# Weight tiles that move on by 16 bytes in SBUF, and up projection tiles streamed backwards

## The chip, the core and the metric

The kernel runs on one core of one Trainium2 chip. The metric is device time in microseconds (us). Three runs of the kernel before gave 872.74, 875.40 and 876.86 us; the median, 875.4 us, is what the prediction is held against. One more execution was profiled.

## The reference

One layer of a diffusion backbone on 512 latent tokens of 1024 channels, with 256 context tokens that only feed the start states of the retention branch. Cut to what matters here:

```python
u = modulate(x, sh1, sc1)                       # layer norm, then adaLN shift and scale
mix = token_mixer(u @ w_in, ...)                # retention and pooling branches, gates, @ w_out
x = post_norm(ALPHA * x + g1 * mix, ln1_g, ln1_b)
u2 = modulate(x, sh2, sc2)
h = (u2 @ w_up).reshape(B, 8, 64, 2 * 2816)     # up projection: 44 feature tiles of 128
h = conv3x3_depthwise(h) + conv_b               # nine taps for every channel
a, b = split(h)
x = post_norm(ALPHA * x + g2 * ((gelu(a) * b) @ w_down), ln2_g, ln2_b)
```

All arithmetic is float32.

## The kernel before, in words

**Split products.** A float32 product is made of three matmuls in the type float32r. A weight tile of 128 rows and 1024 columns is loaded into a buffer `raw`; `split` (L86 to L91) makes two tiles of it: ScalarE (ACT) casts `raw` to `hi` (L89), and VectorE (DVE) or GpSimd (POOL) writes the rest, `lo = raw - hi` (the subtraction stands in a helper, L84). The activations are split in the same way beforehand. `mm3` (L93 to L96) then issues hi by hi (L94), hi by lo (L95) and lo by hi (L96), all summed in one PSUM bank. The tags `hi` and `lo` have two buffers each, which take turns, so every tile of such a tag starts at one of two addresses.

**What uses them.** `feature_mm` (L383) makes one output tile of 128 features by 512 tokens: eight steps over the contraction, 24 matmuls of 512 columns, the weights stationary and the activations streamed. The tiles of the projections for gates and pooling, of the branch projections and most of the up projection are stationary in that way. In the value projection and in most of the down projection the `hi` and `lo` tiles are the streamed side instead. The first stage (`g0_mm`, L339) takes its weights from the same two tags, through a line of its own (L323).

**The order of the work.** Most of the program stands in an order written by hand. In the up projection, the loop near L1001 goes over 44 tiles `i`: it prepares the weights of tile `i + 2` (`up_prep`; each third tile is split into spare room, not into `hi` and `lo`), runs the matmuls of tile `i` (`up_mm`, which calls `feature_mm` for tiles 6 to 43; the first six tiles were prepared earlier and are made in halves of 256 columns), and then starts the 3x3 convolution on the PSUM bank: the centre tap on ACT (L1010), two taps by ACT and POOL (L1013, L936), six by DVE (`tap`, L938). After each second tile there is gelu on ACT, the product of the pair on DVE (`gated`, L987), and the split of the product for the down projection (`act_out`, L991 and L84). There are eight PSUM banks; a bank is free again when the last tap has read it. The down projection follows; its first two weight tiles already need all eight banks.

**Names and lines that matter.** `split` L86, `mm3` L93, `feature_mm` L383, `out_x` L802 (which borrows buffers of the tags `hi` and `lo` for rows of x), `up_mm` L962, `kernel` L1188.

Of the kernel before, what the change touches and what calls it, by code (L numbers as in the profile page):

```python
# [9 lines left out]
F32 = mybir.dt.float32  # L10
F32R = mybir.dt.float32r
# [3 lines left out]
P = 128  # L15
D = 1024
# [4 lines left out]
NKT = D // P  # L21
# [25 lines left out]
def layer_kernel(ctx: ExitStack, tc: tile.TileContext, a: dict):  # L47
    nc = tc.nc
    act, dve, pool, pe, dma = nc.scalar, nc.vector, nc.gpsimd, nc.tensor, nc.sync

    sb = ctx.enter_context(tc.tile_pool(name="sb", bufs=1))
# [5 lines left out]
    def nm(s):  # L57
        count[0] += 1
        return f"{s}_{count[0]}"

    def slot(i, shape, dt=F32):
        return sb.tile(shape, dt, tag=f"S{i}", name=nm(f"S{i}"))
# [7 lines left out]
    def t2(shape=(P, SEQ), dt=F32):  # L70
        return sb.tile(list(shape), dt, tag="t2", bufs=8, name=nm("t2"))
# [8 lines left out]
    def bank():  # L80
        return ps_pool.tile([P, SEQ], F32, tag="ps", name=nm("ps"))

    def sub(eng, out, x, y):
        eng.tensor_tensor(out, x, y, ALU.subtract)  # L84

    def split(raw, shape, eng):  # L86
        hi = sb.tile(list(shape), F32R, tag="hi", bufs=2, name=nm("hi"))
        lo = sb.tile(list(shape), F32R, tag="lo", bufs=2, name=nm("lo"))
        act.copy(hi, raw)  # L89
        sub(eng, lo, raw, hi.bitcast(F32))  # L90
        return hi, lo  # L91

    def mm3(out, sh, sl, mh, ml, first, last):  # L93
        pe.matmul(out, lhsT=sh, rhs=mh, start=first, stop=False)  # L94
        pe.matmul(out, lhsT=sh, rhs=ml, start=False, stop=False)  # L95
        pe.matmul(out, lhsT=sl, rhs=mh, start=False, stop=last)  # L96

    def load(t, src):
        dma.dma_start(t, src)
        return t  # L100
# [63 lines left out]
    def prep(i):  # L164
        _, src, shape, eng = steps[i]
        if src is None:
            return ()
        raw = raw4(shape)
        if isinstance(src, list):
            for k, one in enumerate(src):  # L170
                load(raw[:, k, :], one)
        else:
            load(raw, src)
        return split(raw, shape, eng)
# [30 lines left out]
    def finish_mod(m, j, scale):  # L205
        dve.tensor_scalar(m[:, j:j + 1], m[:, j:j + 1], bada[:, j:j + 1], 1.0 if scale else 0.0, ALU.add, ALU.add)
# [5 lines left out]
    NF0 = (4 + N_G0) * P  # L212
# [39 lines left out]
    def first_prep(kt, raw):  # L252
        w = split(raw, (P, NF0), pool)
        first_mod(kt)
        modulate(mod, kt, 8 + kt, xnT[:, kt, :], uh[:, kt, :], ul[:, kt, :], pool)
        return w
# [63 lines left out]
    finish_mod(mod, 0, False)  # L320
    matvec(8, ada_slot(8), junk)
    finish_mod(mod, 8, True)
    wh, wl = (sb.tile([P, NF0], F32R, tag=t, bufs=2, name=nm(t)) for t in ("hi", "lo"))  # L323
    act.activation(uh[:, 0, :], xnT[:, 0, :], AF.Identity, bias=mod[:, 0:1], scale=mod[:, 8:9])
    for cs, cp in ((lo_half, dve.tensor_copy), (hi_half, act.copy)):
        cp(wh[:, cs], raw0[:, cs])
# [15 lines left out]
    for kt in range(NKT):  # L342
        wh, wl = ready
        if kt == 0:
            g0 = [bank() for _ in range(4)]
            g0_mm(kt, range(0, 4), range(2))
            held += [x_trans(2, 1), x_trans(3, 1)]
            g0_mm(kt, range(0, 4), range(2, 3))
            for h in held:
                act.copy(*h)  # L350
            g0 += [bank() for _ in range(N_G0)]
            ready = split(first_load(1), (P, NF0), pool)
            first_mod(1)
            modulate(mod, 1, 9, xnT[:, 1, :], uh[:, 1, :], ul[:, 1, :], pool)
        elif kt + 1 < NKT:
            ready = first_prep(kt + 1, first_load(kt + 1))
        if kt:
            g0_mm(kt, range(0, 4))
        g0_mm(kt, range(4, 4 + N_G0))
        if kt == 1:  # L360
            silu_cc = load(row(), a["c_ctx"].broadcast_to([P, D]))
        elif kt == 2:
            for hf in range(2):
                cs = slice(hf * SEQ, (hf + 1) * SEQ)
                t = t2()
                act.activation(t, silu_cc[:, cs], AF.Sigmoid)
                dve.tensor_tensor(silu_cc[:, cs], silu_cc[:, cs], t, ALU.mult)
        if kt >= 6:
            load(ctx_raw[:, kt - 6, :], a["ctx"][(kt - 6) * P:(kt - 5) * P, :])
        if kt >= 4:  # L370
            ctx_mod(kt - 4)
# [8 lines left out]
        act.activation(s, ps, AF.Sigmoid)  # L380
        dve.tensor_tensor(gs[:, f, :], ps, s, ALU.mult)

    def feature_mm(wh, wl, nkt, mh, ml):  # L383
        ps = bank()
        for kt in range(nkt):
            mm3(ps, wh[:, kt, :], wl[:, kt, :], mh[:, kt, :], ml[:, kt, :], kt == 0, kt == nkt - 1)
        return ps

    def feature_step(src, nkt, mh, ml, post, eng):
        step(lambda wh, wl: post(feature_mm(wh, wl, nkt, mh, ml)), src, (P, nkt, P), eng)  # L390
# [347 lines left out]
    def br_step(t):  # L738
        def body(wh, wl):
            if t == 0:  # L740
                m1[0] = slot(1, [P, NKT, SEQ])
            ps = feature_mm(wh, wl, NKT, zs[0], zs[1])
            dve.tensor_tensor(m1[0][:, t, :], ps, sg[0][:, t, :], ALU.mult)
            for n in [n for n in range(4) if BR_W[n] == t]:
                prep_out(*divmod(n, 2))

        step(body, a["w_br"][t], (P, NKT, P), dve)

    def bp_step(t):
        def body(wh, wl):  # L750
            if t == 0:
                mm_[0] = slot(2, [P, NKT, SEQ], F32R)
                mm_[1] = slot(5, [P, NKT, SEQ], F32R)
            ps = feature_mm(wh, wl, 4, poolT[:, 0], poolT[:, 1])
            m = t2()
            dve.tensor_tensor(m, ps, sg[1][:, t, :], ALU.mult)
            dve.tensor_tensor(m, m, m1[0][:, t, :], ALU.add)
            act.copy(mm_[0][:, t, :], m)
            sub(pool, mm_[1][:, t, :], m, mm_[0][:, t, :].bitcast(F32))
            for n in [n for n in range(4) if BP_W[n] == t]:  # L760
                prep_out(*divmod(4 + n, 2))

        step(body, a["w_bp"][t], (P, 4, P), dve)
# [25 lines left out]
    mh, ml = mm_  # L789
# [7 lines left out]
    u2h = slot(1, [P, NKT, SEQ], F32R)  # L797
    u2l = slot(8, [P, NKT, SEQ], F32R)

    xr, stats, early = {}, {}, []  # L800

    def out_x(tb):  # L802
        t = xr[tb] = sb.tile([P, D], F32, tag="lo" if tb % 2 else "hi", bufs=2, name=nm("xr"))
        load(t, a["x"][tb * P:(tb + 1) * P, :])
        return act.activation(t, t, AF.Copy, scale=ALPHA)

# [52 lines left out]
    def half(i, hf):  # L859
        ps, wh, wl = early[i]  # L860
        hs = slice(hf * CTX, (hf + 1) * CTX)
        for kt in range(NKT):
            mm3(ps[:, hs], wh(kt), wl(kt), u2h[:, kt, hs], u2l[:, kt, hs], kt == 0, kt == NKT - 1)
# [28 lines left out]
    for tb in range(2):  # L892
        tc.keep_in_program_order(out_x(tb))
# [4 lines left out]
    out_mm(1)  # L898
    out_tr(0)
    out_x(2)  # L900
    early_prep(0, dve)
    out_norm(1)
    out_mm(2)
    out_tr(1)
    out_x(3)
    early_prep(1, dve)
    out_norm(2, lambda: early_prep(2, pool))
# [54 lines left out]
    def up_mm(i):  # L962
        if i < n_early:
            half(i, 1)
            return early[i][0]
        wh, wl = prepped.pop(i)
        return feature_mm(wh, wl, NKT, u2h, u2l)

    srcs, accs = {}, {}

# [29 lines left out]
    for i in range(2 * NFF):  # L1000
        up_prep(i + 2)  # L1001
        ps = up_mm(i)
        if i >= 2 * NFF - 2:
            src = t2()
            act.copy(src, ps)
        else:
            src = ps
        srcs[i] = src
        acc = accs[i] = t2()
        act.activation(acc, src, AF.Identity, bias=convb[:, i:i + 1], scale=convw[:, i, 4:5])  # L1010
        for n in POOL_TAPS:
            hs = t2()
            act.activation(hs, src, AF.Copy, scale=convw[:, i, n:n + 1])  # L1013
            tap(acc, hs, None, *TAPS[n])
        gens = [conv_taps(i, DVE_TAPS[:3])]
        if i:
            gens.insert(0, conv_taps(i - 1, DVE_TAPS[3:]))
        weave(*gens)
        settle(i - 1)
        if i >= 3 and i % 2 == 1:  # L1020
            act_out((i - 3) // 2)
    down0 = down_prep(0, pool)
    i = 2 * NFF - 1
# [29 lines left out]
    for f in range(2, N_FRONT):  # L1053
# [5 lines left out]
        if f >= N_FRONT - 8 and f % 2 == 0:  # L1059
            i = (f - N_FRONT + 8) // 2  # L1060
# [144 lines left out]
```

## Time and profile before

| what | value |
|---|---|
| median of three runs | 875.4 us (872.74 to 876.86) |
| the profiled execution's own time | 874.79 us |
| its span, first to last instruction | 873.0 us |
| TensorE (PE) busy | 821.6 us, 94% |
| VectorE (DVE) busy | 624.4 us, 72% |
| GpSimd (POOL) busy | 444.2 us, 51% |
| ScalarE (ACT) busy | 366.2 us, 42% |
| granted TensorE clock, mean | 0.981 of full |

The profile is of one execution. Busy shares are averages over stages with different limits, so each stage is read by itself. A matmul's own duration overlaps its neighbours' (the array is a pipeline), so its pace is read from the distance of starts. A profile line carries the engine, the line of the program, the operation, the tiles it writes and reads, and shapes; "idle before" names what ended the engine's wait.

### The profile page before, as it was taken

How to read it: one execution, taken by the hardware profiler on the slowest of the kernel's cores; microseconds unless marked ns; L12 is line 12 of the kernel's file. 1: busy time of each engine (PE TensorE's matmuls, PEld its weight loads, DVE VectorE, ACT ScalarE, POOL GpSimd, SP SyncE). 2: the span in 40 equal slices, each digit the busy share in tenths (PEclk: the TensorE clock that was granted, in tenths of full speed). 3: DMA queues.
4: the chain of work that ended last, by engine and by line, in shares of the span. 5: the costliest groups of instructions: out<-in, count | busy, mean ns of one | idle time of the engine just before them, and what ended most of it. 6: DMA issues, size and time to landing. Idle time of an engine off the chain costs nothing.

```text
span 873.0 us, 10556 instructions
## 1 busy us (share of the span) xinstructions
PE 821.6 (94%) x3865; PEld 678.5 (78%) x3865; DVE 624.4 (72%) x959; ACT 366.2 (42%) x575; POOL 444.2 (51%) x304
## 2 busy tenths in 40 slices
PE   6889989999999999998998899999999998799993
PEld 4667878778888888887787898888888776688883
DVE  7899996676267773346757769999999999612138
ACT  4434544121444343233335476666655565223200
POOL 4877411121543230113456878899888886212245
PEclk9999999999999999999999999999999999999997
DMA  9932466767221104344503312222222252224202
GB/s 352 345 105 94 127 207 218 236 226 216 72 73 49 50 1 145 100 154 163 196 1 121 121 50 84 86 96 99 96 97 95 75 169 83 87 97 144 73 1 96
DMA packets 33780, 106.94 MB, mean 122 GB/s; under 512 B 4528, under 2 KB 5312, under 8 KB 33728
## 3 DMA queue, kind: packets, MB, share of 16 engines
q1 hardware_dynamic: 33728, 106.27, 35.6%
q8 instruction: 30, 0.49, 0.2%
q14 instruction: 22, 0.18, 0.1%
HBM read 104.14 MB, written 2.11 MB: 122 GB/s over the span
## 4 chain that ended last, share of the span: by engine, by line
PE 40%; DVE 39%; POOL 8%; DMA 6%; issue 5%; ACT 2%; SPq 0%; DVEq 0%; POOLq 0%; ACTq 0%
DVE t L938 19%; PE ps L96 11%; PE ps L95 11%; PE ps L94 11%; DVE S L84 4%; DMA raw<-in_wada 4%; DVE t L987 3%; POOL lo L84 3%; DVE raw L203 2%; DVE lo L84 2%; PE ps L339 1%; POOL S L84 1%; POOL sm L123 1%; PE ps L608 1%; DVE sm L130 1%
## 5 line engine op out<-in xcount | busy, mean ns | idle before, releaser
L96 PE MATMUL ps<-S,lo 128*128 128x512 f32 (+1 forms) x544 | 212.2, 392 | 5.1 <-DVE lo L84 4.7
L94 PE MATMUL ps<-S,hi 128*128 128x512 f32 (+1 forms) x544 | 213.6, 393 | 2.7 <-ACT hi L89 2.7
L95 PE MATMUL ps<-S,hi 128*128 128x512 f32 (+1 forms) x544 | 212.5, 391 | 0.2 <-POOL S L84 0.2
L84 POOL TENSOR_TENSOR lo<-raw,hi 128x1024 fp32r<-128x1024 f32 (+1 forms) x53 | 134.0, 2530 | 107.2 <-ACT hi L89 105.3
L938 DVE SCALAR_TENSOR_TENSOR t<-ps,convw,t 128x441 f32<-128x441 f32 (+1 forms) x252 | 167.6, 693 | 15.8 <-POOL t L936 11.5
L89 ACT CAST hi<-raw 128x1024 fp32r<-128x1024 f32 (+1 forms) x98 | 98.9, 1009 | 168.2 <-PE ps L95 61.7
L96 PEld LDWEIGHTS ps<-S,lo 128*128 128x128 f32 x544 | 102.8, 189 | 29.8 <-DVE lo L84 6.8
L94 PEld LDWEIGHTS ps<-S,hi 128*128 128x128 f32 x544 | 103.6, 190 | 23.7 <-ACT hi L89 3.1
L936 POOL TENSOR_TENSOR t<-t,t 128x448 f32<-128x448 f32 x88 | 116.7, 1329 | 10.0 <-ACT t L1013 6.2
L95 PEld LDWEIGHTS ps<-S,hi 128*128 128x128 f32 x544 | 103.7, 191 | 21.3 <-POOL S L84 0.6
L95 PE MATMUL ps<-S,S 128*128 128x512 f32 (+1 forms) x308 | 113.8, 370 | 5.4 <-DVE S L84 5.0
L94 PE MATMUL ps<-S,S 128*128 128x512 f32 (+1 forms) x308 | 113.1, 369 | 3.6 <-DVE t L938 3.6
L96 PE MATMUL ps<-S,S 128*128 128x512 f32 (+1 forms) x308 | 113.8, 370 | 0.2 <-POOL S L84 0.2
L84 DVE TENSOR_TENSOR lo<-raw,hi 128x1024 fp32r<-128x1024 f32 (+1 forms) x47 | 61.4, 1307 | 53.0 <-ACT hi L89 53.0
L84 POOL TENSOR_TENSOR S<-raw,S 128x1024 fp32r<-128x1024 f32 x21 | 50.8, 2423 | 68.7 <-ACT S L735 44.5
L95 PE MATMUL ps<-lo,S 128*128 128x512 f32 x208 | 81.6, 392 | 0.7 <-DVE lo L84 0.6
L96 PE MATMUL ps<-hi,S 128*128 128x512 f32 x208 | 81.3, 391 | 0.0
L94 PE MATMUL ps<-hi,S 128*128 128x512 f32 x208 | 79.2, 392 | 0.0
L95 PEld LDWEIGHTS ps<-S,S 128*128 128x128 f32 x308 | 58.9, 191 | 15.6 <-DVE S L84 5.5
L94 PEld LDWEIGHTS ps<-S,S 128*128 128x128 f32 x308 | 58.6, 191 | 13.6 <-DVE t L938 4.0
L96 PEld LDWEIGHTS ps<-S,S 128*128 128x128 f32 x308 | 58.9, 191 | 10.4 <-POOL S L84 1.1
L84 POOL TENSOR_TENSOR S<-t,S 128x512 fp32r<-128x512 f32 (+1 forms) x29 | 44.8, 1557 | 31.2 <-DVE t L220 11.1
(205 smaller groups left out, 1187.3 us busy)
## 6 DMA issues: line engine op xcount, KB each, us to landing
raw<-in_w_up SPq DMA_DIRECT2D x44, 512.0 KB, 3.3
raw<-in_wada SPq DMA_DIRECT2D x32, 512.0 KB, 4.2
raw<-in_w_down SPq DMA_DIRECT2D x22, 512.0 KB, 3.3
S<-in_wada SPq DMA_DIRECT2D x16, 512.0 KB, 6.8
raw<-in_w_first SPq DMA_DIRECT2D x8, 512.0 KB, 7.4
raw<-in_w_v SPq DMA_DIRECT2D x16, 256.0 KB, 3.3
raw<-in_w_ga SPq DMA_DIRECT2D x8, 512.0 KB, 3.4
raw<-in_w_gb SPq DMA_DIRECT2D x8, 512.0 KB, 3.3
```

Source lines behind the costliest of these rows:

```text
L84: eng.tensor_tensor(out, x, y, ALU.subtract)
L89: act.copy(hi, raw)
L94: pe.matmul(out, lhsT=sh, rhs=mh, start=first, stop=False)
L95: pe.matmul(out, lhsT=sh, rhs=ml, start=False, stop=False)
L96: pe.matmul(out, lhsT=sl, rhs=mh, start=False, stop=last)
L123: pool.tensor_scalar(rs, mv[:, 1:2], EPS, None, ALU.add)
L130: dve.bn_stats(st[:, hf, :], src[:, hf * SEQ:(hf + 1) * SEQ])
L203: dve.scalar_tensor_tensor(out_junk, raw, 1.0, silu_c, ALU.mult, ALU.mult, accum_out=mod[:, j:j + 1])
L339: pe.matmul(g0[f], lhsT=w[:, f * P:(f + 1) * P], rhs=m[:, kt, :], start=kt == 0 and i == 0, stop=kt == NKT - 1 and i == 2)
L936: pool.tensor_tensor(o, o, i, ALU.add)
L938: dve.scalar_tensor_tensor(o, i, w, o, ALU.mult, ALU.add)
L987: dve.tensor_tensor(accs[2 * f], accs[2 * f], accs[2 * f + 1], ALU.mult)
```

## The change

It does four things.

1. `split` takes its two tiles from a new helper, `halves`. It allocates 1152 columns (4608 bytes) in place of 1024 and hands out a piece that starts at a shift. The shift grows by 4 elements, 16 bytes, from one pair to the next, and comes back to 0 after 32 pairs; `hi` and `lo` of a pair have the same shift. The first stage's pair comes from it too.
2. `feature_mm` has a new argument, `way`. For odd tiles of the up projection it is `back`, which reverses the last axis: the streamed operands and the PSUM output both run from column 511 down to 0. That is tiles 7, 9 and so on to 43: 19 tiles, 456 matmuls. The stationary weights are not reversed, so each PSUM element receives what it received before.
3. `out_x` allocates its rows of x with 1152 columns, since it shares the two tags, and uses the first 1024.
4. The room for this (four buffers, 512 bytes more in each partition for each) comes from `dynamic_dma_scratch_size=1024`. The kernel before has 16384 bytes reserved at the start of SBUF; every other tile starts 15360 bytes lower now, and those after the two tags 13312 bytes lower.

```diff
+    shift = [0]
+
+    def halves(shape):
+
+        shift[0] = (shift[0] + 4) % P
+        n = int(np.prod(shape[1:]))
+        out = []
+        for tag in ("hi", "lo"):
+            t = sb.tile([P, D + P], F32R, tag=tag, bufs=2, name=nm(tag))[:, shift[0]:shift[0] + n]
+            out.append(t.rearrange("p (k c) -> p k c", k=shape[1]) if len(shape) == 3 else t)
+        return out
+
     def split(raw, shape, eng):
-        hi = sb.tile(list(shape), F32R, tag="hi", bufs=2, name=nm("hi"))
-        lo = sb.tile(list(shape), F32R, tag="lo", bufs=2, name=nm("lo"))
+        hi, lo = halves(shape)
...
+    def back(t):
+        return t[:, ::-1]
...
-    wh, wl = (sb.tile([P, NF0], F32R, tag=t, bufs=2, name=nm(t)) for t in ("hi", "lo"))
+    wh, wl = halves((P, NF0))
...
-    def feature_mm(wh, wl, nkt, mh, ml):
+    def feature_mm(wh, wl, nkt, mh, ml, way=lambda t: t):
         ps = bank()
         for kt in range(nkt):
-            mm3(ps, wh[:, kt, :], wl[:, kt, :], mh[:, kt, :], ml[:, kt, :], kt == 0, kt == nkt - 1)
+            mm3(way(ps), wh[:, kt, :], wl[:, kt, :], way(mh[:, kt, :]), way(ml[:, kt, :]), kt == 0, kt == nkt - 1)
...
-        t = xr[tb] = sb.tile([P, D], F32, tag="lo" if tb % 2 else "hi", bufs=2, name=nm("xr"))
+        t = xr[tb] = sb.tile([P, D + P], F32, tag="lo" if tb % 2 else "hi", bufs=2, name=nm("xr"))[:, 0:D]
...
-        return feature_mm(wh, wl, NKT, u2h, u2l)
+        return feature_mm(wh, wl, NKT, u2h, u2l, back if i % 2 else lambda t: t)
...
-    nc = _bacc.Bacc("TRN2", target_bir_lowering=False, num_devices=1)
+    nc = _bacc.Bacc("TRN2", target_bir_lowering=False, num_devices=1, dynamic_dma_scratch_size=1024)
```

No compute instruction and no transfer is added, removed or moved on any engine. What differs in the built program beside addresses and steps is 21 waits. On DVE, in the up projection, the first tap of a backward tile waited for POOL alone (`ps` is the tile's PSUM bank, `t` its accumulator). Before:

```order
L938 SCALAR_TENSOR_TENSOR t_792_5395<-ps_5370,convw,t_792_5395 128x7x63 [waits DVE_49] x2
L938 SCALAR_TENSOR_TENSOR t_799_5441<-ps_5416,convw,t_799_5441 128x7x63 [waits Pool_49]
L938 SCALAR_TENSOR_TENSOR t_799_5441<-ps_5416,convw,t_799_5441 128x7x63 [waits DVE_49]
L938 SCALAR_TENSOR_TENSOR t_799_5441<-ps_5416,convw,t_799_5441 128x8x63 [waits DVE_49] x2
L938 SCALAR_TENSOR_TENSOR t_799_5441<-ps_5416,convw,t_799_5441 128x7x63 [waits DVE_49] x2
```

The same place in the changed program:

```order
L952 SCALAR_TENSOR_TENSOR t_792_5395<-ps_5370,convw,t_792_5395 128x7x63 [waits DVE_49] x2
L952 SCALAR_TENSOR_TENSOR t_799_5441<-ps_5416,convw,t_799_5441 128x7x63 [waits PE_49,Pool_49]
L952 SCALAR_TENSOR_TENSOR t_799_5441<-ps_5416,convw,t_799_5441 128x7x63 [waits DVE_49]
L952 SCALAR_TENSOR_TENSOR t_799_5441<-ps_5416,convw,t_799_5441 128x8x63 [waits DVE_49] x2
L952 SCALAR_TENSOR_TENSOR t_799_5441<-ps_5416,convw,t_799_5441 128x7x63 [waits DVE_49] x2
```

A wait for PE has come in ahead of the first tap. The value it waits for is that of the backward tile's last matmul, for which ACT waits too before it starts the accumulator `t`, and POOL after ACT. There are 18 of them (in the last pair the taps read an SBUF copy, not PSUM). Such pairs of waits stand in the kernel before as well, at the first taps of tiles 1 to 5, on DVE:

```order
L938 SCALAR_TENSOR_TENSOR t_617_4067<-ps_3816,convw,t_617_4067 128x7x63 [waits PE_49,Pool_49]
L938 SCALAR_TENSOR_TENSOR t_614_4032<-ps_3791,convw,t_614_4032 128x8x63 [waits DVE_49]
L938 SCALAR_TENSOR_TENSOR t_617_4067<-ps_3816,convw,t_617_4067 128x7x63 [waits DVE_49]
L938 SCALAR_TENSOR_TENSOR t_614_4032<-ps_3791,convw,t_614_4032 128x8x63 [waits DVE_49]
L938 SCALAR_TENSOR_TENSOR t_617_4067<-ps_3816,convw,t_617_4067 128x8x63 [waits DVE_49]
L938 SCALAR_TENSOR_TENSOR t_620_4106<-ps_3874,convw,t_620_4106 128x7x63 [waits PE_49,Pool_49]
```

These rows are the same in both programs. The other three of the 21 stand on PE, at the first matmul of the down projection into each of three banks that held backward tiles: they wait for DVE as before, and now also for the PE's own matmuls of those tiles.

## Rows read from the trace of the kernel before

**Rows 1.** The page's head and busy time by engine.
```profile
span 873.0 us, 10556 instructions
PE 821.6 (94%) x3865; PEld 678.5 (78%) x3865; DVE 624.4 (72%) x959; ACT 366.2 (42%) x575; POOL 444.2 (51%) x304
```
**Rows 2.** Busy time by stretch: from:to, length, engines with counts, PEclk, DMA, GB/s.
```profile
0.00:511.00 511.00, 482.85 (x2365) 400.25 (x2366) 346.47 (x601) 199.62 (x341) 205.62 (x157) 0.98 0.42 146
524.00:729.00 205.00, 204.04 (x891) 166.54 (x890) 199.37 (x258) 122.73 (x181) 182.73 (x108) 1.00 0.30 100
729.00:754.00 25.00, 16.84 (x65) 12.83 (x64) 24.43 (x29) 10.71 (x16) 10.55 (x7) 0.93 0.14 49
754.00:764.00 10.00, 9.50 (x35) 7.75 (x36) 2.97 (x4) 2.62 (x3) 1.53 (x1) 0.83 0.46 157
764.00:843.00 79.00, 79.00 (x350) 65.45 (x350) 13.05 (x12) 19.71 (x20) 16.71 (x9) 1.00 0.26 87
```
**Rows 3.** Chain of work that ended last, 524 to 754 us, shares by line.
```profile
by line: DVE t L938 67.1%; DVE S L84 13.9%; DVE t L987 11.9%; issue 4.3%; POOL t L936 1.3%; POOL lo L84 0.8%; DVE lo L84 0.5%; ACT hi L89 0.5%; DVEq L987 0.1%; POOLq L84 0.0%; ACT S L991 0.0%; ACTq L1010 0.0%
```
**Rows 4.** DVE timeline, up projection: start, length, engine, line, operation.
```profile
621.93 1.38 DVE L987 TENSOR_TENSOR t<-t,t 128x512 f32<-128x512 f32 x1
...
633.63 1.36 DVE L987 TENSOR_TENSOR t<-t,t 128x512 f32<-128x512 f32 x1
...
639.56 5.66 DVE L938 SCALAR_TENSOR_TENSOR t<-ps,convw,t 128x441 f32<-128x441 f32 x8
645.32 1.36 DVE L987 TENSOR_TENSOR t<-t,t 128x512 f32<-128x512 f32 x1
```
**Rows 5.** PE timeline, up projection, matmuls of 512 columns.
```profile
600.42 0.39 PE L94 MATMUL ps<-S,hi 128*128 128x512 f32 x1
...
601.10 0.39 PE L94 MATMUL ps<-S,hi 128*128 128x512 f32 x1
```
**Rows 6.** PE timeline, start of the down projection; in brackets idle before, releaser.
```profile
726.87 0.50 PE L95 MATMUL ps<-S,S 128*128 128x512 f32 x1 [0.37 <-POOL S L84]
...
733.28 0.50 PE L94 MATMUL ps<-S,S 128*128 128x512 f32 x1 [3.62 <-DVE t L938]
...
734.32 0.63 PE L94 MATMUL ps<-S,S 128*128 128x512 f32 x1
734.75 0.63 PE L95 MATMUL ps<-S,S 128*128 128x512 f32 x1
...
754.50 0.80 PE L95 MATMUL ps<-S,S 128*128 128x512 f32 x1 [5.04 <-DVE S L84]
```
**Rows 7.** DVE timeline, first taps of the up projection, tiles 0 to 5.
```profile
510.21 13.54 DVE L938 SCALAR_TENSOR_TENSOR t<-ps,convw,t 128x441 f32<-128x441 f32 x22 [11.06 <-POOL t L936]
```
**Rows 8.** PE timeline, up tiles made in halves of 256 columns.
```profile
504.75 0.28 PE L96 MATMUL ps<-S,t 128*128 128x256 f32 x1
504.87 0.29 PE L94 MATMUL ps<-S,t 128*128 128x256 f32 x1
```
**Rows 9.** Groups by line and shape: busy us, mean ns, idle before.
```profile
L84 POOL TENSOR_TENSOR lo<-raw,hi 128x1024 fp32r<-128x1024 f32 x51 | 130.8, 2565 | 105.3 <-ACT hi L89 105.3
...
L459 POOL TENSOR_TENSOR t<-t 128x527 f32<-128x527 f32 x4 | 5.9, 1474 | 50.7 <-ACT t L451 50.7
...
L89 ACT CAST hi<-raw 128x512 fp32r<-128x512 f32 x8 | 4.9, 618 | 12.7 <-PE ps L95 12.7
...
L451 ACT COPY t<-ps 128x512 f32<-128x512 f32 x4 | 2.3, 577 | 0.0
```
**Rows 10.** Busy time of instructions on tile hi by stretch, then tile lo.
```profile
0.00:511.00 511.00, 311.62 (x1025) 193.54 (x1025) 54.48 (x42) 62.03 (x63) 60.36 (x23) 0.98 0.42 146
729.00:873.00 144.00, 60.93 (x192) 36.49 (x192) 7.34 (x6) 12.49 (x12) 14.41 (x6) 0.94 0.24 82
...
0.00:511.00 511.00, 192.22 (x512) 97.33 (x512) 54.06 (x41) 60.36 (x23) 0.98 0.42 146
729.00:873.00 144.00, 37.63 (x96) 18.32 (x96) 7.34 (x6) 14.41 (x6) 0.94 0.24 82
```

## The prediction

> **What bounds the kernel now.** The page's busy times come first [rows 1]: PE is at work in 821.6 of 873.0 us, so a change that makes matmuls slower or faster should show. The stretches then say where that is less direct [rows 2]. From 524 to 729 us, nearly the whole up projection, PE is busy in 204.04 of 205 us, but DVE in 199.37 too. The chain of waits decides between them [rows 3]: from 524 to 754 us it runs on DVE lines for over 90%, and no matmul line is in it. The DVE timeline gives the pace [rows 4]: the product of a pair of tiles starts at 621.93, 633.63 and 645.32 us, so DVE takes 11.69 us for two tiles. PE starts a matmul of 512 columns each (601.10 - 600.42) / 3 = 0.2267 us [rows 5], or 48 x 0.2267 = 10.88 us for two tiles. PE runs ahead of DVE and later pays it back: at the start of the down projection it stands still for 0.37, 3.62 and 5.04 us [rows 6], 9.0 us in all, and after the two long stops it runs at half clock for a while (PEclk 0.93 over 25 us and 0.83 over 10 us: 25 x 0.07 x 2 and 10 x 0.17 x 2, some 3.4 us each at 1.2 GHz in place of 2.4, worth 1.7 us of matmuls each) [rows 2]. So in the up projection DVE sets the end, and PE has 9.0 us, with the clock 12.4 us, that a slower up projection would use up first. Then PE is the bound: it is busy in 79.00 of the 79 us from 764 us on [rows 2].
>
> **The change, part by part.** No operation is added and none moved, so the sum is made of prices per operation.
>
> *Waits on DVE.* 18 backward tiles get a wait for PE ahead of their first tap. What it waits for is the tile's last matmul, which the wait for POOL implies already: POOL adds onto an accumulator that ACT made after that same matmul. So nobody waits longer; only the cost of one more wait is in question, and it would lie on the chain, since DVE is the bound there. The kernel before has five such waits among the 22 first taps, and these run 13.54 us without a gap, 0.615 us each [rows 7], against 5.66 / 8 = 0.708 us in a stretch without one [rows 4]. So I take 0. The upper bound is the worst gap that a wait makes in the steady state, from the end of the eight taps (639.56 + 5.66 = 645.22) to 645.32: 0.10 us [rows 4], 18 x 0.10 = 1.8 us. The three new waits on PE are for its own matmuls of tiles long done, at a place where it is waiting for DVE anyway [rows 6]: 0.
>
> *Shifted tiles, on the engines that fill them.* ACT now writes `hi` some way into a buffer: it already writes 512 columns at an offset of 32 bytes in 577 ns, against 618 ns for 512 columns at a buffer's start [rows 9]. POOL's sums over tokens shifted by one element take 1474 / 527 = 2.80 ns an element, its `lo` 2565 / 1024 = 2.50 [rows 9]. If all of that difference came from the offset, a `lo` would take 0.3 us more, and the 24 of the up projection 7.4 us, in a stretch where POOL has 205 - 182.73 = 22.3 us to spare [rows 2]. DVE's taps work on pieces that start one column in. I take 0 for the three.
>
> *Shifted tiles as stationary weights.* In halves of 256 columns a weight load keeps up with a matmul each 0.12 us [rows 8], so at 0.2267 us it has over 0.1 us to spare. Those rows read weights from tiles `t`, which in the built program start 64 bytes further into a 512-byte line-up from one buffer to the next; no row shows 16 bytes. Only tile 0's halves, 48 matmuls on `hi` and `lo`, have no such slack: twice the load would be 48 x 0.12 = 5.8 us, 0 at the other end. I take 0, as those `t` rows are the nearest.
>
> *Shifted tiles as the streamed side.* Matmuls on `hi` number 1025 and on `lo` 512 up to 511 us, and 192 and 96 from 729 us on [rows 10]; in the later stretch all are streams. A price per stream is between nothing and one more of the gap of 13 ns that stands between two matmuls now (0.2267 us less 512 columns at 2.4 GHz, 0.2133): 288 x 0.0133 = 3.8 us there. I take 0.
>
> *Backward streams.* This is the large unknown: 456 matmuls read SBUF and write PSUM downwards, and no row shows one. The lower bound is 0: the same 512 elements of one row and one bank are touched, next to each other; a gain is worth nothing here, because DVE sets the pace. The upper bound is the nearest row of a slow stream, 512 columns at 1.2 GHz, whose starts lie 734.75 - 734.32 = 0.43 us apart (512 / 1.2 GHz is 0.427) [rows 6]: 456 x (0.427 - 0.2267) = 91.3 us. I take 0, because the order of elements within a row gives the array nothing else to do, and keep the other end as a rival. A price up to 9.0 us / 456 = 20 ns a matmul disappears in PE's stops; I count none.
>
> *Lower addresses, less room reserved at the start.* All transfers are issued from SP's queue; I count 0.
>
> The sum is 0 on the profiled execution's 874.79 us, which lies 0.6 us under the median of 875.4. With a little for the 18 waits I predict 875.5 us.
>
> **A rule that speaks against it.** The upper bound above is read from rows alone. The Trainium skill, "Advanced Engine Details and Errata", section Memory Cachelines, has a mechanism for it: PSUM has lines of 8 bytes, two float32 values, and "Any non-contiguous AP significantly slows down matmuls". If step -1 counted as non-contiguous, that would be the half pace; if only neighbourhood counts (the same section asks that every two consecutive elements be contiguous), it would be the 0 that I took. The same skill, "SBUF — State Buffer", Specifications (TRN2), gives SBUF lines of 16 bytes and asks for two hits on each; by that a shift of 16 bytes and a downward read cost nothing. No run here shows either for a negative step.
>
> **The rivals.**
>
> *Backward streams go at half pace (slower).* Place: 19 tiles from 524 us on. A pair would take 24 x 0.2267 + 24 x 0.427 = 15.7 us on PE against DVE's 11.69, so PE becomes the bound; this decides as soon as a backward matmul costs over 27 ns more (12.4 us / 456). Of the 91.3 us, 9.0 replace stops and 3.4 come back as clock: +78.9, some 954 us. For it: nothing in the trace streams downwards, and hardware may pair neighbours only upwards. Against it: nothing in the rows; the data is dense either way. Chance 0.17.
>
> *A small price.* 40 to 65 ns for a backward matmul (18 to 30 us less 12.4), or the bounds of the shift together with the 1.8 us of DVE: 880 to 892 us. Chance 0.10.
>
> *The 13 ns gap goes away (faster).* If it came from weights and streams that start on the same addresses time after time, moving them would save it in the 1025 + 512 + 192 + 96 = 1825 matmuls outside the DVE-bound stretch: 24.3 us, 851 us; half of them, 863. Against it: the gap is the same where the weights are `t` tiles at other starts (0.12 us less 256 columns at 2.4 GHz, 0.1067, is 13 ns again) [rows 8]. Chance 0.05.
>
> That the change does not do what it says can be left out: the built program has the 456 matmuls with step -1 on stream and output.
>
> **How the numbers follow.** No effect 0.68, half pace 0.17, small price 0.10, gap gone 0.05. A measurement of this kernel tells about 0.5%, 4.4 us, from no change (the three runs span 4.1 us); so faster 0.05, same 0.68, slower 0.27. The range takes in the first case with its scatter, the small price up to 892 and the lesser savings down to 866; left out are the half pace and most of the saving, 0.2 in all.
>
> **What would show it.** Right: matmuls of backward tiles start 0.227 us apart like the forward ones; DVE's pair still takes 11.7 us; PE stops near 733 and 754 us for 9 us in all; POOL's `lo` stays near 2565 ns and ACT's `hi` at its length. Half pace: starts 0.43 us apart in every second up tile, no stop at the start of the down projection, DVE idle in the up projection. Small price: the stops shrink and the end moves. Gap gone: 0.213 us between matmuls of stages on `hi` and `lo`. The prediction is wrong if any of these prices is paid on the chain.

## The result and the profile after

Three runs of the changed kernel took 883.67, 883.78 and 884.08 us, median 883.78. The kernel before has 875.4: the ratio is 1.0101, 95% interval 1.0062 to 1.0140. A second measurement, six runs of the change against 22 of before, gives 882.69 us to 873.77, ratio 1.0086 (1.0069 to 1.0104), +8.9 us. So the change makes the kernel about 1% slower. The forecast of no effect, 875.5 us, was wrong. The range of 866 to 892 held the time, and what happened has the size of the rival called a small price, though not its mechanism; that the range reached so far is in part luck.

The profiled execution of the changed kernel took 884.08 us, its span is 9.3 us longer than before, and the granted clock is alike (0.983, before 0.981). In the changed kernel 14 has to be added to the numbers of most lines: `mm3` is L108 to L110, the tap L952, POOL's convolution add L950, the product of a pair L1001; the kernels that move `S` (below) have 8 more. Head and busy times of the page after, to set beside [rows 1]:

```profile
span 882.3 us, 10577 instructions
PE 830.0 (94%) x3865; PEld 676.8 (77%) x3865; DVE 628.5 (71%) x959; ACT 366.0 (41%) x575; POOL 442.3 (50%) x304
```

PE has 8.4 us more work and DVE 4.1 us, with the same number of instructions on each. The stretches after, columns as in [rows 2]:

```profile
0.00:511.00 511.00, 480.46 (x2324) 392.48 (x2325) 346.53 (x599) 195.60 (x335) 201.07 (x153) 0.99 0.42 145
524.00:729.00 205.00, 205.00 (x883) 165.35 (x882) 200.08 (x256) 122.46 (x180) 176.23 (x106) 1.00 0.29 95
...
764.00:843.00 79.00, 79.00 (x338) 64.24 (x337) 13.64 (x12) 20.55 (x21) 14.34 (x6) 0.98 0.31 104
```

In stretches where PE is busy throughout it gets through fewer matmuls: 883 in 205 us where it was 891, and 338 in 79 where it was 350. Of the last 12 the clock, 0.98 in place of 1.00, takes some 7 (79 x 0.02 / 0.227 us, an estimate). The same is read from starts. PE timeline after, up projection, the first matmul of some tiles of 24:

```profile
610.87 0.40 PE L108 MATMUL ps<-S,hi 128*128 128x512 f32 x1
...
616.47 0.39 PE L108 MATMUL ps<-S,S 128*128 128x512 f32 x1
...
622.07 0.40 PE L108 MATMUL ps<-S,hi 128*128 128x512 f32 x1
...
633.28 0.39 PE L108 MATMUL ps<-S,S 128*128 128x512 f32 x1
...
638.76 0.40 PE L108 MATMUL ps<-S,hi 128*128 128x512 f32 x1
```

The tile from 610.87 us streams forwards against weights shifted by 144 bytes: 5.60 us / 24 = 233 ns a matmul. The one from 616.47 streams backwards against unshifted weights: 233 ns too. The one from 633.28 is forward and unshifted: 5.48 / 24 = 228 ns, near the 226.7 of before [rows 5]. In the whole trace a matmul of 512 columns with a shifted `hi` or `lo` on either side takes, averaged by position, 229 to 235 ns to the next one when both run forwards; halves of 256 columns on shifted weights take 117 ns, before 120.

Two such tiles are 11.2 us of PE, still under DVE's 11.7. So in the up projection the slower PE should be hidden, and PE's stops at the start of the down projection should pay. They hardly shrink, from 9.0 to 8.0 us in all (PE timeline after; before 0.37, 3.62 and 5.04 us [rows 6]):

```profile
734.58 0.50 PE L109 MATMUL ps<-S,S 128*128 128x512 f32 x1 [0.29 <-POOL S L84]
...
740.99 0.79 PE L108 MATMUL ps<-S,S 128*128 128x512 f32 x1 [3.62 <-DVE t L952]
...
762.24 0.50 PE L109 MATMUL ps<-S,S 128*128 128x512 f32 x1 [4.12 <-DVE S L84]
```

Those stops stem from DVE's last tiles, and PE waits there whatever its pace was before. What DVE loses counts in full, and it does lose something, in one place. Both engines in the timeline of before, then of after: the products of some pairs, POOL's two adds ahead of one of them, and behind it a `lo` on POOL and DVE's subtraction for the split of the product (L84, `S<-t,S`).

```profile
552.98 1.62 DVE L987 TENSOR_TENSOR t<-t,t 128x512 f32<-128x512 f32 x1
...
561.07 3.02 POOL L936 TENSOR_TENSOR t<-t,t 128x448 f32<-128x448 f32 x2
...
562.39 0.68 DVE L987 TENSOR_TENSOR t<-t,t 128x512 f32<-128x512 f32 x1
...
564.75 3.01 POOL L84 TENSOR_TENSOR lo<-raw,hi 128x1024 fp32r<-128x1024 f32 x1 [0.66 <-ACT hi L89]
564.82 0.68 DVE L84 TENSOR_TENSOR S<-t,S 128x512 fp32r<-128x512 f32 x1
...
569.05 0.68 DVE L987 TENSOR_TENSOR t<-t,t 128x512 f32<-128x512 f32 x1
...
610.24 1.37 DVE L987 TENSOR_TENSOR t<-t,t 128x512 f32<-128x512 f32 x1
```

```profile
558.06 1.63 DVE L1001 TENSOR_TENSOR t<-t,t 128x512 f32<-128x512 f32 x1
...
566.14 2.39 POOL L950 TENSOR_TENSOR t<-t,t 128x448 f32<-128x448 f32 x2
...
567.49 1.58 DVE L1001 TENSOR_TENSOR t<-t,t 128x512 f32<-128x512 f32 x1
...
570.75 2.40 POOL L84 TENSOR_TENSOR lo<-raw,hi 128x1024 fp32r<-128x1024 f32 x1 [2.23 <-ACT hi L100]
570.82 2.88 DVE L84 TENSOR_TENSOR S<-t,S 128x512 fp32r<-128x512 f32 x1
...
577.26 1.57 DVE L1001 TENSOR_TENSOR t<-t,t 128x512 f32<-128x512 f32 x1
...
618.27 1.35 DVE L1001 TENSOR_TENSOR t<-t,t 128x512 f32<-128x512 f32 x1
```

Call the product at 552.98 us (558.06 after) A and the one at 610.24 (618.27) B; it is the sixth product behind A. A comes 5.1 us later after the change, B 8.0: 2.95 us are lost between them (57.26 us, after 60.21), and that between the second and the third product of each fence (6.66 us, after 9.77). There the two engines change roles, twice. Before, POOL's two adds take 3.02 us and DVE's product 0.68; after, the adds take 2.39 and the product 1.58. Before, POOL's `lo` takes 3.01 us and DVE's subtraction 0.68; after, the `lo` takes 2.40 and the subtraction 2.88. Each time one of them waits inside its instruction for the other. So of the 3.1 us lost there, the product has 0.9 and the subtraction 2.2. (The third product takes 0.9 us longer too, but from there to B DVE needs no longer than before, 41.0 us for 41.2.)

**The loss in three pieces:** 5.1 us up to A, 2.95 from A to B, and from B to the end of the span 264.03 us for 262.76, 1.3 more; in all 9.3.

### The profile page after: what moved, and what is told of

Same layout as the page of the kernel before. It is cut to its first block, busy times and chain, and to the rows that moved or that the text cites. A ratio compares the mean times of both kernels' runs of the same rounds, so it can differ in the third digit from the quotient of the medians.

```text
span 882.3 us, 10577 instructions
## 1 busy us (share of the span) xinstructions
PE 830.0 (94%) x3865; PEld 676.8 (77%) x3865; DVE 628.5 (71%) x959; ACT 366.0 (41%) x575; POOL 442.3 (50%) x304
## 4 chain that ended last, share of the span: by engine, by line
PE 41%; DVE 38%; issue 7%; POOL 6%; DMA 5%; ACT 2%; SPq 0%; DVEq 0%; POOLq 0%; ACTq 0%
DVE t L952 18%; PE ps L110 12%; PE ps L108 12%; PE ps L109 12%; DVE S L84 5%; DMA raw<-in_wada 4%; DVE t L1001 3%; DVE lo L84 2%; DVE raw L217 2%; POOL lo L84 2%; PE ps L353 1%; POOL S L84 1%; POOL sm L137 1%; PE ps L622 1%; DVE sm L144 1%
## 5 line engine op out<-in xcount | busy, mean ns | idle before, releaser
L110 PE MATMUL ps<-S,lo 128*128 128x512 f32 (+1 forms) x544 | 213.5, 394 | 5.5 <-DVE lo L84 5.3
L108 PE MATMUL ps<-S,hi 128*128 128x512 f32 (+1 forms) x544 | 214.7, 395 | 2.2 <-ACT hi L100 2.2
L84 POOL TENSOR_TENSOR lo<-raw,hi 128x1024 fp32r<-128x1024 f32 (+1 forms) x53 | 133.2, 2514 | 115.5 <-ACT hi L100 113.6
L952 DVE SCALAR_TENSOR_TENSOR t<-ps,convw,t 128x441 f32<-128x441 f32 (+1 forms) x252 | 167.5, 693 | 17.2 <-POOL t L950 12.9
L100 ACT CAST hi<-raw 128x1024 fp32r<-128x1024 f32 (+1 forms) x98 | 98.9, 1009 | 176.0 <-PE ps L109 65.2
L110 PEld LDWEIGHTS ps<-S,lo 128*128 128x128 f32 x544 | 102.5, 189 | 31.9 <-DVE lo L84 8.1
L108 PEld LDWEIGHTS ps<-S,hi 128*128 128x128 f32 x544 | 102.7, 189 | 25.2 <-ACT hi L100 2.6
L950 POOL TENSOR_TENSOR t<-t,t 128x448 f32<-128x448 f32 x88 | 115.8, 1319 | 10.0 <-ACT t L1027 6.9
L108 PE MATMUL ps<-S,S 128*128 128x512 f32 (+1 forms) x308 | 114.4, 373 | 3.6 <-DVE t L952 3.6
L110 PE MATMUL ps<-S,S 128*128 128x512 f32 (+1 forms) x308 | 114.4, 372 | 0.0
L84 DVE TENSOR_TENSOR lo<-raw,hi 128x1024 fp32r<-128x1024 f32 (+1 forms) x47 | 61.4, 1306 | 55.1 <-ACT hi L100 55.1
L84 POOL TENSOR_TENSOR S<-raw,S 128x1024 fp32r<-128x1024 f32 x21 | 50.7, 2416 | 69.7 <-ACT S L749 45.2
L110 PE MATMUL ps<-hi,S 128*128 128x512 f32 x208 | 82.6, 397 | 0.0
L108 PE MATMUL ps<-hi,S 128*128 128x512 f32 x208 | 80.3, 397 | 0.0
L109 PEld LDWEIGHTS ps<-S,S 128*128 128x128 f32 x308 | 59.5, 193 | 15.1 <-DVE S L84 4.5
L108 PEld LDWEIGHTS ps<-S,S 128*128 128x128 f32 x308 | 59.4, 194 | 14.0 <-DVE t L952 4.0
L110 PEld LDWEIGHTS ps<-S,S 128*128 128x128 f32 x308 | 59.5, 193 | 9.8
L84 POOL TENSOR_TENSOR S<-t,S 128x512 fp32r<-128x512 f32 (+1 forms) x29 | 44.9, 1562 | 30.7 <-DVE t L234 11.1
```

The source lines that it names most:

```text
L950: pool.tensor_tensor(o, o, i, ALU.add)
L952: dve.scalar_tensor_tensor(o, i, w, o, ALU.mult, ALU.add)
```

## The experiments

All kernels are the changed one with an edit; the interval of a ratio is 95%.

**The shift alone.**

```diff
-        return feature_mm(wh, wl, NKT, u2h, u2l, back if i % 2 else lambda t: t)
+        return feature_mm(wh, wl, NKT, u2h, u2l)
```

> The shift of 16 bytes a pair without the backward streams. Theory A (the pace of a 512-column matmul hangs on the distance, modulo 256 bytes, between the start of its stream and the start of the weights loaded beside it: 226.7 ns at distance 0, 229 to 234 ns at others): starts 231 to 234 ns apart in all stages on hi and lo, 226.7 at distances 0 and 256, and 881 to 884 us, nearly all of the loss. Theory C (the backward streams are the loss): starts 227 ns apart, 874 to 877 us.

Measured: 879.69 us, ratio 1.0059 (1.0037 to 1.0082), +5.1 us. So the shift alone costs more than half of it, without any backward tile. From A to B it takes 57.31 us (556.67 to 613.98), as before. PE timeline of this kernel, starts of three tiles with weights at 16, 0 and 32 bytes, and the next one's:

```profile
674.76 0.39 PE L108 MATMUL ps<-S,hi 128*128 128x512 f32 x1
...
680.20 0.39 PE L108 MATMUL ps<-S,S 128*128 128x512 f32 x1
...
685.65 0.39 PE L108 MATMUL ps<-S,hi 128*128 128x512 f32 x1
...
691.24 0.40 PE L108 MATMUL ps<-S,hi 128*128 128x512 f32 x1
```

The distances over 24 give 226.7, 227.1 and 232.9 ns: not each shift costs. Positions here and below are the addresses in the built programs, modulo 256 bytes.

**The backward tiles alone.**

```diff
-        shift[0] = (shift[0] + 4) % P
+        shift[0] = 0
```

> The backward streams without the shift: every pair of weight tiles starts at the same place as before. Theory A: backward matmuls start 233.5 ns apart, forward ones 226.7, and since VectorE sets the pace of most of the up projection the time is 875 to 878 us. Theory C: 881 to 884 us.

Measured: 874.97 us, ratio 1.0010 (0.9987 to 1.0033): no difference that can be told. PE timeline, first matmuls of a backward tile, a forward one and the next:

```profile
597.30 0.40 PE L108 MATMUL ps<-S,hi 128*128 128x512 f32 x1
...
602.90 0.40 PE L108 MATMUL ps<-S,hi 128*128 128x512 f32 x1
...
608.36 0.40 PE L108 MATMUL ps<-S,S 128*128 128x512 f32 x1
```

Backward 5.60 / 24 = 233 ns, forward 5.46 / 24 = 227.5. The price is there, 449 matmuls at 233.5 ns on average, some 6.8 ns x 456 = 3.1 us of PE, and hidden. But the 2.95 us of DVE between A and B are there as well (60.11 us), with the roles changed as in the kernel after:

```profile
558.79 2.39 POOL L950 TENSOR_TENSOR t<-t,t 128x448 f32<-128x448 f32 x2
...
560.14 1.59 DVE L1001 TENSOR_TENSOR t<-t,t 128x512 f32<-128x512 f32 x1
```

**The tiles moved by 256 bytes in place of 16, nothing backward.**

```diff
-        shift[0] = (shift[0] + 4) % P
+        shift[0] = (shift[0] + 64) % P
...
-        return feature_mm(wh, wl, NKT, u2h, u2l, back if i % 2 else lambda t: t)
+        return feature_mm(wh, wl, NKT, u2h, u2l)
```

> The same helper, but the shift goes on by 256 bytes (64 elements) from pair to pair, no backward streams. Theory A: distance 0 modulo 256 everywhere, starts 226.7 ns apart, 873 to 877 us. A theory that any move of the tiles, or the smaller reserved room, costs: 881 us or more.

Measured: 873.86 us, ratio 0.9994 (0.9977 to 1.0012). PE timeline, two tiles in a row, 5.44 us / 24 = 226.7 ns:

```profile
550.05 0.39 PE L108 MATMUL ps<-S,hi 128*128 128x512 f32 x1
...
555.49 0.39 PE L108 MATMUL ps<-S,hi 128*128 128x512 f32 x1
```

So moving tiles, the lower addresses of all others and the smaller room reserved at the start cost nothing that shows (by the interval, some 1 us at most); the 16 bytes do.

**Where the 16 bytes hurt: fixed positions.** Five kernels with one profiled run each, nothing backward. Both `hi` and `lo` and the large tiles `S`, among them the streamed activations, at 16 bytes; `hi` and `lo` alone at 16; `S` alone at 16; `S` at 16 with `hi` and `lo` at 240; and `S` at 16 with `hi` and `lo` moving on by 16. The edit that moves `S`, in short:

```diff
-        return sb.tile(shape, dt, tag=f"S{i}", name=nm(f"S{i}"))
+        t = sb.tile([P, 4096 + P], dt, tag=f"S{i}", name=nm(f"S{i}"))[:, 4:4 + n]
...
```

The first moves `S` and sets the shift:

```diff
-        shift[0] = (shift[0] + 4) % P
+        shift[0] = 4
```

> All weight tiles hi and lo and all large tiles S that they are multiplied with stand 16 bytes past a multiple of 512, none moves, no backward streams. Theory A: every distance is 0, starts 226.7 ns apart, 873 to 877 us. Theory B (each operand that does not start on a 256-byte boundary costs by itself): 232 ns or more everywhere, also between tiles S, and 885 us or more.

Measured, both at 16: 883.17 us. If only the distance between weights and stream counted, this would have been free. It is not: all matmuls of 512 columns in the up projection take 231.1 ns.

The second has that shift, and `S` as it was.

> The tiles hi and lo alone stand 16 bytes past a multiple of 512, always; the large tiles S stay on multiples; no backward streams. Theory A: distance 16, starts 231 to 234 ns apart with hi and lo, 226.7 between tiles S, 881 to 885 us. Theory B: the same here; the two differ in the run where both kinds are shifted.

Measured, weights at 16: 882.40 us (before, on the same chip, 875.05).

The third moves `S`, with `shift[0] = 0`.

> The large tiles S alone stand 16 bytes past a multiple of 512; hi and lo stay on multiples; no backward streams. Theory A: between tiles S 226.7 ns (distance 0 although both are shifted); with hi and lo, at distance 496 or 16, 229 to 234 ns; 879 to 885 us. Theory B: between tiles S 233 ns or more, with hi and lo 232.

Measured, `S` at 16: 883.25 us. Tiles with both sides in `S` take 232.9 ns, those with `hi` and `lo` at 0 231.6: an aligned partner doesn't help.

The fourth moves `S`, with:

```diff
-        shift[0] = (shift[0] + 4) % P
+        shift[0] = 60
```

> The large tiles S stand 16 bytes past a multiple of 512, hi and lo 240 bytes past one: neither is on a boundary of 256, the sum of the two is. Theory B (each read that does not start on a boundary of 256 bytes costs, whatever the other does): 230 to 234 ns with hi and lo, 231 to 233 between tiles S, 881 to 885 us. Theory A2 (stream and weight load are read in opposite directions, and the pace hangs on the sum of their starts): 226.7 ns where hi and lo are the weights, 231 or more between tiles S.

Measured, 16 and 240: 880.58 us (before 873.77). PE timeline: a tile of the up projection that streams `S` at 16 against weights at 240, and in the down projection 16 matmuls that stream `hi` and `lo` at 240 against `S` at 16.

```profile
554.62 0.40 PE L116 MATMUL ps<-S,hi 128*128 128x512 f32 x1
...
560.22 0.40 PE L116 MATMUL ps<-S,hi 128*128 128x512 f32 x1
...
766.44 0.39 PE L116 MATMUL ps<-hi,S 128*128 128x512 f32 x1
...
770.07 0.39 PE L117 MATMUL ps<-lo,S 128*128 128x512 f32 x1
```

The first is 5.60 / 24 = 233 ns, the second 3.63 / 16 = 226.9. With the sides swapped the same pair of positions is free, though neither lies on 256 bytes: neither the sum of the two positions decides, nor each read by itself.

The fifth moves `S` and keeps the shift of the change.

> The large tiles S stand 16 bytes past a multiple of 512, and hi and lo move on by 16 bytes from pair to pair, as in the changed kernel; no backward streams. So every position of hi and lo is met against a partner at 16, as weights and as stream. Theory D (the pace hangs on the two positions together, and the pair of boundaries is one free pair among several): some positions give 227 ns against a partner at 16, others 230 to 235, and as streams others than as weights. Theory B (each read off a boundary costs by itself): no position gives under 229 ns where hi and lo are the weights. 880 to 885 us either way.

Measured: 879.84 us (before 875.91). PE timeline, tiles with weights at 16 (`hi`), at 16 (`S`) and at 32:

```profile
674.73 0.39 PE L116 MATMUL ps<-S,hi 128*128 128x512 f32 x1
...
680.32 0.40 PE L116 MATMUL ps<-S,S 128*128 128x512 f32 x1
...
685.92 0.39 PE L116 MATMUL ps<-S,hi 128*128 128x512 f32 x1
...
691.36 0.39 PE L116 MATMUL ps<-S,hi 128*128 128x512 f32 x1
```

233, 233 and 226.7 ns. With the stream at 0 it was weights at 32 that cost and at 16 that didn't; with the stream at 16 it is the other way round. Averaged over this trace, some positions of the weights are free (48 and 208: 227.3 ns) and some cost in full (96: 233.3).

Position is not even all of it. PE timeline of the kernel with weights at 16 and stream at 0:

```profile
522.72 0.40 PE L110 MATMUL ps<-S,lo 128*128 128x512 f32 x1
...
533.45 0.40 PE L108 MATMUL ps<-S,S 128*128 128x512 f32 x1
...
538.93 0.39 PE L108 MATMUL ps<-S,hi 128*128 128x512 f32 x1
...
549.81 0.39 PE L108 MATMUL ps<-S,S 128*128 128x512 f32 x1
```

The 46 matmuls from 522.72 to 533.45 take 233 ns each, the 48 from 538.93 to 549.81 226.7, at the same positions. So one pair of positions off the 256 bytes can run at either pace; with both on them every pair seen stays at 227 or near it.

**Reading or writing backwards.** Without shift, every fourth tile reads its stream downwards only and every fourth writes PSUM downwards only, so the tokens of these tiles come out mirrored.

```diff
-            mm3(way(ps), wh[:, kt, :], wl[:, kt, :], way(mh[:, kt, :]), way(ml[:, kt, :]), kt == 0, kt == nkt - 1)
+            mm3(out(ps), wh[:, kt, :], wl[:, kt, :], way(mh[:, kt, :]), way(ml[:, kt, :]), kt == 0, kt == nkt - 1)
...
+        return feature_mm(wh, wl, NKT, u2h, u2l, back if i % 4 == 1 else lambda t: t, back if i % 4 == 3 else lambda t: t)
```

> No shift. Of the odd up tiles 7 to 43, those with i % 4 == 1 read their streams downwards and write PSUM upwards, those with i % 4 == 3 read upwards and write downwards; so the features of these tiles come out with the tokens mirrored, and the output is not the reference's. Theory A (two reads of SBUF that get into each other's way): 233.5 ns where the read is downwards, 226.7 where only the PSUM write is. A theory that the downward PSUM write costs: the other way round.

Measured: 878.64 us. PE timeline, a tile read downwards, a forward one, one written downwards, and the next:

```profile
577.12 0.40 PE L108 MATMUL ps<-S,S 128*128 128x512 f32 x1
...
582.73 0.40 PE L108 MATMUL ps<-S,hi 128*128 128x512 f32 x1
...
588.18 0.39 PE L108 MATMUL ps<-S,hi 128*128 128x512 f32 x1
...
593.62 0.39 PE L108 MATMUL ps<-S,S 128*128 128x512 f32 x1
```

234, 227 and 227 ns. The SBUF read makes the price, the PSUM write none. A stream read downwards also starts at its last element, 4 bytes below a multiple of 256, and no run has one that starts on the 256 bytes. So whether the order costs, or only the start, isn't shown. That weights read downwards as well would repair it wasn't tried.

**The change again, and its backward tiles early or late.**

The change itself, without an edit:

> The changed kernel again, beside the kernel before on one chip. Theory S (shift and backward streams add up: 5.1 us of the shift alone plus about 3 us, by which VectorE's subtractions and products of the up projection got longer when the tiles' pace changed): 881 to 884 us. If the backward streams cost nothing in time: 879 to 880 us.

Measured: +8.9 us, as told above; from A to B 60.21 us, to the hundredth as in the first profile.

No shift, and only tiles 7 to 15 backwards:

```diff
-        shift[0] = (shift[0] + 4) % P
+        shift[0] = 0
...
+        return feature_mm(wh, wl, NKT, u2h, u2l, back if i % 2 and i < 17 else lambda t: t)
```

> No shift; only the five odd tiles 7 to 15 are streamed backwards, those that run while VectorE and GpSimd are not yet in their steady pattern. Theory S: all of the backward streams' cost in time is here, 875.5 to 877.5 us, with VectorE's L84 and L1001 groups longer by 2 to 3 us in the up projection. Theory N (backward streams cost no time, differences are scatter): 873.5 to 875.5 us.

Measured: 874.23 us, ratio 1.0015 (0.9993 to 1.0036). From A to B 60.26 us.

No shift, and only tiles 17 to 43 backwards:

```diff
-        shift[0] = (shift[0] + 4) % P
+        shift[0] = 0
...
+        return feature_mm(wh, wl, NKT, u2h, u2l, back if i % 2 and i >= 17 else lambda t: t)
```

> No shift; only the fourteen odd tiles 17 to 43 are streamed backwards. Matmuls of these tiles start 233.5 ns apart, 336 of them, 2.3 us of TensorE's time. Theory S: hidden behind VectorE's 11.7 us for a pair, 873.5 to 875.5 us. A theory that TensorE's time counts in the end: 876 to 877 us.

Measured: 874.44 us, ratio 1.0002 (0.9988 to 1.0015). From A to B 57.15 us; POOL and DVE keep the roles of before:

```profile
558.42 3.03 POOL L950 TENSOR_TENSOR t<-t,t 128x448 f32<-128x448 f32 x2
...
559.76 0.67 DVE L1001 TENSOR_TENSOR t<-t,t 128x512 f32<-128x512 f32 x1
```

So late backward tiles are hidden, as forecast for all. Times alone can't tell for the early ones: 2.95 us is 1.0034, inside the interval of the kernel with early tiles and at the edge of that with all. The traces can. The three pieces in every profiled execution but four (the other kernels with `S` moved, 57.3 to 57.4 from A to B), from DVE's products and the spans:

| kernel | start to A | A to B | B to end |
|---|---|---|---|
| before | 552.98 | 57.26 | 262.8 |
| moved by 256 bytes | 553.61 | 57.29 | 263.2 |
| late backward tiles | 550.35 | 57.15 | 262.6 |
| early backward tiles | 554.50 | 60.26 | 263.3 |
| all backward tiles | 550.73 | 60.11 | 262.4 |
| read or written downwards | 553.13 | 60.28 | 263.5 |
| weights at 16 bytes | 558.78 | 57.31 | 264.5 |
| shift alone | 556.67 | 57.31 | 264.6 |
| the change | 558.06 | 60.21 | 264.0 |
| the change again | 558.34 | 60.21 | 264.8 |

The middle column has two values and nothing between: some 60.2 us in all five executions with early backward tiles, 57.15 to 57.41 in the nine others. The first scatters by 4 us among kernels with the same pace of PE, and the time at half clock on the way doesn't explain it: up to A it is some 17 us in all before, 10 in the change and 7 with all tiles backwards. On average the six kernels without 16-byte positions reach A at 552.6 and have 263.0 us from B on; the three with the moving 16 bytes 557.7 and 264.5. The last column holds with the clock alike: where both falls to half clock at the start of the down projection last 6.8 us, it is 263.3 with early backward tiles and 263.5 with tiles read or written downwards, but 264.8 in the change again.

## Why the forecast failed, point by point

**What bounds the kernel** held: DVE's pair takes 11.66 us after (618.27 to 629.93 us), PE is the bound in the last stretch. By its own sign the forecast is wrong: prices are paid on the chain. What I did with the bound was too narrow: I spent the argument on the up projection, the one place where PE's pace hardly matters.

**Shifted tiles as weights and as streams**, each taken at 0, is the step that failed first. I argued that a weight load has over 0.1 us to spare beside a matmul of 512 columns, and took rows of 256-column halves as the nearest. Slack isn't the question: the pace of the matmuls themselves changes, and by the runs not in halves but with 512 columns. Also, my bounds covered only tile 0's halves and the 288 streams of the end; the 1537 matmuls on `hi` and `lo` up to 511 us [rows 10] got no price. Measured from the trace after: the 1425 of 512 columns there that ran at full clock without a wait start 232.0 ns apart on average, before 227.4, which is 6.6 us. Of it some 5 us arrive at A (5.1 between the averages above, among kernels that scatter by 4); where the rest goes was not traced. For the 281 of the down projection it is 5.5 ns each, 1.5 us, and 1.5 arrive. This is the +5.1 us of the shift alone, within the scatter. The row that could have warned me was in the trace of before: eleven matmuls of 512 columns with both sides in `t` tiles, which start off the 256 bytes, lie some 233 ns apart.

**Backward streams** taken at 0: the reason was wrong and the consequence mostly right. A downward read does cost (233.5 ns), by its order or by its start, and a downward write doesn't. The 3.1 us are below the 9.0 us of stops, as the text allowed, and the late tiles show them hidden. The half pace, at 427 ns, did not come. By the Trainium skill, "Advanced Engine Details and Errata", Memory Cachelines, a non-contiguous PSUM access slows matmuls significantly; with step -1 the measured 227 ns show none of it, so for neighbours in falling order that rule doesn't speak. The same section of the Trainium skill asks for two hits on each SBUF line of 16 bytes. By the prediction's reading of it both the shift and the downward read were free; the 233 ns show a price that this rule doesn't account for.

**Waits on DVE**, 0 with a bound of 1.8 us: the bound is broken, not by the length of a wait: from A to the next product DVE takes 9.41 to 9.45 us in all fourteen traces, with the new wait or without. Between A and B, DVE loses 2.95 us once, in a product and the subtraction behind it, which wait for POOL where before POOL waited for them. Read to the nanosecond from the traces, POOL's second add starts 75 to 101 ns ahead of DVE's product in the nine executions with forward early tiles, and 106 to 122 ns in the five with backward ones. So a few tens of ns go with who waits: POOL, which has time, or DVE, which is the bound. The second meeting can't be told in this way: POOL's `lo` starts 57 to 69 ns ahead of the subtraction in the nine and 60 to 64 in the five, and yet it goes the way of the first in every execution. The Trainium skill has the mechanism: "SBUF — State Buffer", the section on two separate sides, says that DVE with two SBUF inputs and GpSimd share a port pair as an exclusive lock: one has it for its whole instruction, and the other blocks. The trace agrees: 0.68 or 1.58 us for the product, with 3.02 or 2.39 for the adds; 0.68 or 2.88 for the subtraction, with 3.01 or 2.40 for the `lo`. That section of the Trainium skill gives the pair to whichever starts first; by the recorded starts that is POOL in all fourteen, at both meetings, so the traces don't show what decides. What moves POOL's add is not settled either. POOL's `lo` just ahead of the adds takes 2.40 to 2.41 us in place of 2.42 to 2.44, and in the same stretch lie both the added wait on DVE and the backward streams; they were not separated.

**Engines that fill the shifted tiles, lower addresses**: 0 was right, though the 577 and 618 ns that I set side by side are of unlike operations, a copy out of PSUM and a cast out of SBUF. `hi` and `lo` on the page after, all shapes together, take 1009 and 2514 ns, before 1009 and 2530, and the shift by 256 bytes costs nothing in time:

```profile
L84 POOL TENSOR_TENSOR lo<-raw,hi 128x1024 fp32r<-128x1024 f32 (+1 forms) x53 | 133.2, 2514 | 115.5 <-ACT hi L100 113.6
...
L100 ACT CAST hi<-raw 128x1024 fp32r<-128x1024 f32 (+1 forms) x98 | 98.9, 1009 | 176.0 <-PE ps L109 65.2
```

**The sum, mended:** 5.1 us for the shift and 2.95 for the lost meetings are 8.05, inside the interval of the second measurement (0.69% to 1.04% of 873.77, 6.0 to 9.1 us) and of the first. **The rivals:** the small price came about by its second wording, the shift and DVE together, and not by 40 to 65 ns for a backward matmul. But the places differ: its bounds for the shift were tile 0's halves, which cost nothing, and the 288 streams of the end; its bound for DVE was a gap at each of 18 waits, and what came was two meetings with POOL in one place. That the gap of 13 ns goes away had the wrong sign: with starts on 256 bytes the pace is at its best of all that was seen, and moving them by 16 bytes mostly widens the gap to some 20 ns.

Open stays why a start off the 256 bytes costs, since neither distance, sum nor each position alone foretells it, whether a downward read costs by its order or by its start, what turns the two meetings with POOL, and why backward tiles alone don't show their 2.95 us clearly in the median. No version tried beats the kernel before.

## What to carry to other kernels

Keep both operands of long float32r matmuls at starts that are multiples of 256 bytes, and price a pace change of a few ns over all stages where TensorE is the bound, not only where the edit is. Where DVE sets the pace and shares its work with GpSimd, look for places where their instructions start within some 100 ns of each other: here an edit that reversed the streams of nearby tiles, with a wait that came along, turned two such meetings around and cost 2.95 us. A stretch between two fixed instructions of the critical engine, read from every trace, could here tell 3 us that run times couldn't.

## What the runs showed that I had not expected

- The pace of a float32r matmul of 512 columns has at least two values, 226.7 and about 233 ns, and a given pair of positions can run at either: with weights at 16 bytes two tiles took 233 ns and those after 538.93 us 226.7.
- Reading the stream downwards, from a start 4 bytes below a multiple of 256, costs 6.8 ns a matmul, writing PSUM downwards nothing (227 ns).
- Halves of 256 columns don't pay: 117 ns on weights at 208 bytes, 120 before.
- How DVE and POOL meet is reproducible: it falls one way in the five executions with early backward tiles (60.11 to 60.28 us from A to B) and the other way in the nine without (57.15 to 57.41).
- The larger part of that loss, 2.2 us, is in the subtraction behind the product: 2.88 us in place of 0.68.
